# First layer: stored parts of x^T, gains folded into the split of plain weights, and gains of weight sums moved from VectorE to ScalarE

## Chip, cores and metric

The kernel runs on one core of a Trainium2 chip. The metric is the device time of the launch in microseconds (us), the median of several runs. One more run is profiled; its trace gives each instruction's engine, start and length. Short names of the engines: PE is TensorE (PEld its weight loads), DVE is VectorE, ACT is ScalarE, POOL is GpSimd, SP is the queue that issues DMAs.

## What is computed

A trunk of two layers over 2048 frames of width 1024, in float32. Only the first layer is touched:

```
h = rms_norm(x, g)                       # g: a_norm_g, 1024 values
u, v, z = split(h @ w_in, 3)             # w_in: 1024 x 6144
u = gelu(u)
v = layer_norm(gelu(v), ln_g, ln_b)
mixed = einsum('hts,bgshc->bgthc', masked w_s, v in blocks of 128 frames) + b_s
x = x + (u * mixed * silu(z)) @ w_out
```

The second layer (shared K/V, chunked band attention, its output projection) and the final norm follow.

## The kernel before, in words

**Numbers in two parts.** Every float32 operand of a matmul is split into a rounded part `hi` and a remainder `lo`, and a product is three matmuls (`hi*hi`, `hi*lo`, `lo*hi`; lines 114 to 116). A split is an ACT copy that rounds (line 438) and a DVE subtraction (line 441).

**Seven products instead of eight.** `h @ w_in` is cut into column groups `n`: `n = 0, 1` are the halves of `v`, `n = 2` to `5` hold 512 columns of `u` beside 512 of `z`; a last group `"o"` is the projection by `w_out`. In each group the 2 x 2 block product is formed from seven products `ph`, in the order 1, 2, 6, 5, 7, 4, 3, each over eight pairs of row blocks `j`. One (n, ph, j) is a *step*: twelve matmuls of 128 x 512 on PE into one PSUM tile `P`. Groups 0 and 1 share the steps of products 1 and 2 (24 matmuls each). `run_steps` walks through all steps in order; what belongs to other steps (loads, weights, mixing, transposes) is attached to a step number by `at`, `put` and `add_t`.

**Left operands (tiles `S`, six of them).** For group 0 they are made from x^T, scaled by each row's norm (`prep0`), and for products 3 to 7 the split tiles are also stored in DRAM (`hsd`, 512 KB each) by `s_split`. Groups 1 to 5 load products 3 to 7 from `hsd` with `s_load`. For products 1 and 2, groups 2 to 5 load 128 x 512 of plain x^T (tile `xq`, 256 KB, line 676) and split it again (`s_plain`, `s_parts`); the row's norm is then applied at the eviction. `prep` of a step is emitted three steps ahead (`LOOK`).

**Right operands (tiles `T`, eight of them).** `make_t` makes the weights of a product in three functions: `load` (tiles `rw`, tag `raw`, four buffers), `combine` and `finish`. The norm's weight `ga` is multiplied in by `gain`. Products 1, 2 and 3 use one plain block of the weights: two ACT multiplications of 512 columns in place (line 489), then the split: one ACT copy and one DVE subtraction of 1024 columns. Groups 0 and 1 differ: product 1 is `fused` (ACT multiplies straight into `hi`, line 520, and one DVE instruction forms `raw*g - hi`, line 521), and product 2 has its gain on DVE (line 487). Product 6 needs a sum: POOL forms `t1` as a difference of two blocks, `gain` on DVE (line 487) scales it, and POOL subtracts it from a gained third block.

**Who else works on DVE and ACT.** Product 1 is evicted from PSUM by ACT (line 601), the others by DVE (lines 596, 607, 628). For groups 2 to 5 the mixing runs during products 1, 2, 6 and 5: `va` is loaded from DRAM, normalised by four DVE instructions (lines 877 and 878), split (`vh`, `vl`), multiplied on PE (`mx`) and evicted by ACT (line 901). Gated results go through gelu/tanh on ACT, products on DVE or POOL (lines 907, 925, 931, 932), and are transposed on PE (`ty`, line 912).

**What sets the order.** The program is written step by step; a scheduler at compile time then orders each engine's instructions by that priority, by the buffers and by estimated readiness, so a load can be issued well ahead of its step. Each engine and the SP queue then run strictly in their order. `behind`, `in_order` and `paced` add edges that hold one instruction behind another; `last["square"]` is the instruction (the square of a row, line 772) behind which the splits of groups 0 and 1 for products 6, 4, 5 and 7 are held. `row_rep` (line 782) spreads a row's norm for a PE transposition (`rbc`, line 785) that scales x^T in group 0.

Of the kernel before, what the change touches and what calls it, by code (L numbers as in the profile page):

```python
# [33 lines left out]
def trunk_kernel(  # L34
# [20 lines left out]
    nc = tc.nc  # L55
# [331 lines left out]
    with ExitStack() as actx:  # L387
# [3 lines left out]
        NJ = NB // 2  # L391
        hsd = {
            (ph, j): dram.tile([P, 2, 512], F32, name=f"hsd{ph}_{j}")
            for ph in range(3, 8) for j in range(NJ)
        }
        s1d = [dram.tile([P, 512], F32, name=f"s1d{j}") for j in range(NJ)]
        vd = {
# [49 lines left out]
        def comb(o, x_, y_, op=sub):  # L447
            for c in (slice(0, 512), slice(512, 1024)):
                nc.gpsimd.tensor_tensor(o[:, c], x_[:, c], y_[:, c], op=op)
            return o  # L450

        def make_t(n, ph, src, nq, where, chain_of):


            out = [None] * nq
            vs = [None] * nq
            rows = {}
            need = {
                1: [(0, 0)], 2: [(1, 0)], 3: [(1, 1)], 7: [(1, 1), (0, 1)], 4: [(1, 0)],
                6: [(0, 1), (0, 0), (1, 1)], 5: [],  # L460
            }[ph]
            made = n == "o" and ph in (4, 5, 6, 7)
            fused = n in (0, 1) and ph == 1
            if made:
                need = [ph]

            def load(q):
                if made:
                    t = sh.tile([P, 1024], F32, tag="raw", name=f"rw{n}_{ph}_{q}", bufs=4)
                    nc.sync.dma_start(t[:], wod[ph, q][:])  # L470
                    vs[q] = t[:]
                    return
                for r, c in need:
                    t = sh.tile([P, 1024], F32, tag="raw", name=f"rw{n}_{ph}_{r}{c}{q}", bufs=4)
                    nc.sync.dma_start(t[:], src[r, c, q])
                    rows[r, c, q] = t[:]

            def combine(q):
                if made:
                    return  # L480

                def gain(t, r, dve=n in (0, 1) and ph == 2):
                    for i in range(2) if n != "o" and not fused else ():
                        t_ = t[:, i * 512 : i * 512 + 512]
                        k = r * 4 + q * 2 + i
                        if dve:
                            nc.vector.tensor_scalar(t_, t_, ga[:, k : k + 1], None, op0=mul)
                        else:
                            nc.scalar.mul(t_, t_, ga[:, k : k + 1])  # L489
                    return t  # L490

                def raw(r, c):
                    return gain(rows.pop((r, c, q)), r)

                if ph in (1, 2, 3):
                    v = raw(*need[0])
                elif ph == 7:
                    v = raw(1, 1)
                    comb(v, v, raw(0, 1))
                elif ph == 4:  # L500
                    v = chain[n](q)
                    comb(v, raw(1, 0), v)
                elif ph == 5:
                    v = chain[n](2 + q)
                else:
                    if q == 0:
                        chain[n] = chain_of()
                    b22 = raw(1, 1)
                    t1 = comb(chain[n](2 + q), rows.pop((0, 1, q)), rows.pop((0, 0, q)))
                    v = comb(chain[n](q), b22, gain(t1, 0, True))  # L510
                vs[q] = v

            def finish(q):
                out[q] = where(q)
                if fused:
                    for i in range(2):
                        c_ = slice(i * 512, i * 512 + 512)
                        g_ = ga[:, 2 * q + i : 2 * q + i + 1]
                        hi, lo, src = out[q][0][:, c_], out[q][1][:, c_], vs[q][:, c_]
                        nc.scalar.mul(hi, src, g_)  # L520
                        nc.vector.scalar_tensor_tensor(  # L521
                            lo, src, g_, hi.bitcast(F32), op0=mul, op1=sub
                        )
                    return
                ins = split(*out[q], vs[q])
                if n in (0, 1) and ph in (6, 4, 5, 7):
                    behind(ins, last["square"])

            return out, (load, combine, finish)
# [106 lines left out]
        def s_views(t):  # L636
            return [(t[:, 0, k, :], t[:, 1, k, :]) for k in range(4)]
# [8 lines left out]
        def s_parts(n, ph, j, rows):  # L646

            t = s_tile(f"S{n}_{ph}_{j}")
            split(
                t[:, 0].rearrange("p k c -> p (k c)"), t[:, 1].rearrange("p k c -> p (k c)"),  # L650
                rows, "S",
            )
            return t
# [21 lines left out]
                r, c = plain[ph]  # L675
                nc.sync.dma_start(t, xt[2 * j + r, :, c * 512 : c * 512 + 512])

        def s_plain(n, ph, j):
            return s_views(s_parts(n, ph, j, xq.pop((n, ph, j))))


        late = []
        now = [0]
# [95 lines left out]

        def row_rep(blk):  # L780
            d = rep[blk] = acc_tile(f"rp{blk}")[:, 0:P]
            nc.scalar.mul(d, ones[:], rs[:, blk : blk + 1])

        def row_spread(blk):
            tpose(rbc[:, blk, 0], rep.pop(blk), ident[:])
# [177 lines left out]
        for n in range(6):  # L963
            for ph in PH:
                where = in_t(n, ph)
                s = start.get((n, ph), start[0, ph])
                if n == 0 or (n == 1 and ph in (1, 2)):
                    offs = ((-6, 1), (-5, 1), (-4, 1))
                elif n > 2:
                    o = -13 if ph == 6 else -5  # L970
                    offs = ((o, 1), (o, 1), (-5, 1))
                elif ph == 6:
                    offs = ((-13, 3), (-11, 3), (-5, 1))
                elif ph == 4:
                    offs = ((-14, 1), (-12, 1), (-5, 1))
                else:
                    offs = ((-8, 1), (-6, 1), (-5, 1))
                if n == 1 and ph in (1, 2):
                    where = in_big(n, ph, ("hh",) if ph == 1 else ("hl",))
                    offs = ((-5, 1), (-4, 1), (-3, 1))  # L980
                if n == 5 and ph == 3:
                    where = in_big(n, ph, ("hl",))
                add_t(ts, s, n, ph, w_a[n], 2, where, chain_in(n, "hl" if n else "hh"), offs)
# [37 lines left out]
        for n in range(2, 6):  # L1021
# [3 lines left out]
            for r, offs in ((0, (5, 9, 13, 17)), (1, (22, 25, 28, 31))):  # L1025
                for q, o in enumerate(offs):
# [4 lines left out]
                    if r == 0:  # L1031
                        for i in range(2):
                            j = 2 * q + i
                            at(b + 16 + j, lambda n=n, j=j: merge_u(n, j))

        def prep_in(n, ph, j):
            if n == 0:
                return prep0(ph, j)
            if ph in (1, 2):
                return s_plain(n, ph, j)  # L1040
            return s_load(ph, j, n)

        def act_in(s, n, ph, j, views):
# [7 lines left out]
                    evict(m, ph, j, ps, done_uz, uz_c22(m))  # L1051

        for n, ph in start:
            if (n == 0 and ph in (4, 5)) or (n in range(2, 6) and ph < 3):
                for j in range(NJ):
                    at(start[n, ph] + j - LOOK - 2, lambda a=(n, ph, j): xq_load(*a))

# [1011 lines left out]
```

## Time and profile before

| | before |
|---|---|
| median of 3 runs | 2674.11 us (2672.39 to 2676.29) |
| profiled execution, its own time | 2671.83 us |
| its span in the trace | 2670.1 us |
| PE busy | 2595.7 us (97%) |
| DVE busy | 1972.7 us (74%) |
| ACT busy | 1438.0 us (54%) |
| POOL busy | 907.5 us (34%) |
| granted PE clock, mean | 0.994 |
| DMA | 695.14 MB, mean 260 GB/s |

PE is busy nearly all the time, so what there is to be had lies in its idle stretches and in stretches with a lower granted clock. Matmuls overlap, so a row of 0.39 us stands for a matmul that starts about 0.23 us after the one before. All times inside a run are counted from the start of the span. The first layer's column groups 0 to 5 lie between about 8 and 1055 us.

### The profile page before, as it was taken

How to read it: one execution, taken by the hardware profiler on the slowest of the kernel's cores; microseconds unless marked ns; L12 is line 12 of the kernel's file. 1: busy time of each engine (PE TensorE's matmuls, PEld its weight loads, DVE VectorE, ACT ScalarE, POOL GpSimd, SP SyncE). 2: the span in 40 equal slices, each digit the busy share in tenths (PEclk: the TensorE clock that was granted, in tenths of full speed). 3: DMA queues.
4: the chain of work that ended last, by engine and by line, in shares of the span. 5: the costliest groups of instructions: out<-in, count | busy, mean ns of one | idle time of the engine just before them, and what ended most of it. 6: DMA issues, size and time to landing. Idle time of an engine off the chain costs nothing. (4 is left out here: it accounts for less than half of the span.)

```text
span 2670.1 us, 37974 instructions
## 1 busy us (share of the span) xinstructions
PE 2595.7 (97%) x12752; PEld 2161.6 (81%) x12752; DVE 1972.7 (74%) x3060; ACT 1438.0 (54%) x2539; POOL 907.5 (34%) x875
## 2 busy tenths in 40 slices
PE   9899999999999899999999999999999999999997
PEld 7688787878778788888877877888888888888886
DVE  5885795875967968667767766777778777877677
ACT  7453373554734734343356555666666565666564
POOL 3812154242341412302334424334333232232245
PEclk9999999999999999999999999999999999999999
DMA  8799978878778668968867487688788767775667
GB/s 302 282 352 342 362 277 325 305 257 291 259 265 279 230 228 305 331 213 263 297 237 247 163 273 236 220 259 263 247 263 266 232 198 227 254 227 162 200 221 253
DMA packets 273858, 695.14 MB, mean 260 GB/s; under 512 B 28928, under 2 KB 68864, under 8 KB 273664
## 3 DMA queue, kind: packets, MB, share of 16 engines
q1 hardware_dynamic: 273664, 692.72, 76.2%
q8 instruction: 102, 1.67, 0.3%
q14 instruction: 92, 0.75, 0.1%
HBM read 513.82 MB, written 168.30 MB: 255 GB/s over the span
## 5 line engine op out<-in xcount | busy, mean ns | idle before, releaser
L114 PE MATMUL P<-T,S 128*128 128x512 f32 x1248 | 497.0, 398 | 16.7 <-DVE c L607 7.9
L116 PE MATMUL P<-T,S 128*128 128x512 f32 x1248 | 490.1, 393 | 0.4 <-DVE S L441 0.4
L115 PE MATMUL P<-T,S 128*128 128x512 f32 x1248 | 489.1, 392 | 0.3 <-DVE T L521 0.3
L1489 POOL TENSOR_SCALAR pr<-pr,ns 128x640 f32<-128x640 f32 (+4 forms) x256 | 207.7, 812 | 528.5 <-DVE ns L1488 437.5
L114 PE MATMUL pj<-hh_b,wh_b 128*128 128x512 f32 x768 | 319.6, 416 | 0.1
L116 PE MATMUL pj<-hh_b,wl_b 128*128 128x512 f32 x768 | 303.8, 396 | 0.9 <-DVE wl_b L232 0.8
L115 PE MATMUL pj<-hl_b,wh_b 128*128 128x512 f32 x768 | 302.5, 394 | 0.0
L1485 ACT ACTIVATE pr<-pr,ns 128x640 f32<-128x640 f32 (+4 forms) x256 | 195.5, 764 | 188.8 <-DVE ns L1478 187.9
L114 PEld LDWEIGHTS P<-T,S 128*128 128x128 f32 x1248 | 236.3, 189 | 69.2 <-issue 10.2
L116 PEld LDWEIGHTS P<-T,S 128*128 128x128 f32 x1248 | 235.7, 189 | 52.1 <-DVE S L441 1.3
L115 PEld LDWEIGHTS P<-T,S 128*128 128x128 f32 x1248 | 236.4, 189 | 45.4 <-DVE T L521 0.6
L1510 DVE TENSOR_TENSOR pt<-tp,pt 128x640 fp32r<-128x640 f32 (+4 forms) x256 | 188.5, 736 | 44.5 <-ACT pt L1509 41.9
L1478 DVE CUSTOM_DVE_ANT_0 pr<-s,bias 128x640 f32<-128x640 f32 (+4 forms) x256 | 188.1, 735 | 33.8 <-PE s L1470 28.8
L1509 ACT CAST pt<-tp 128x640 fp32r<-128x640 f32 (+4 forms) x256 | 158.7, 620 | 54.8 <-PE tp L1505 50.4
L1505 PE MATMUL tp<-ident,pr 128*128 128x128 f32 x1120 | 166.5, 274 | 9.4 <-DVE pt L1510 7.8
L116 PEld LDWEIGHTS pj<-hh_b,wl_b 128*128 128x128 f32 x768 | 144.5, 188 | 35.4 <-DVE wl_b L232 3.0
L1505 PEld LDWEIGHTS tp<-ident,pr 128*128 128x128 f32 x1120 | 130.6, 141 | 44.3 <-issue 15.8
L1530 PEld LDWEIGHTS pv<-pt,V 128*128 128x128 f32 x896 | 143.0, 188 | 21.0 <-ACT pt L1509 3.6
L114 PEld LDWEIGHTS pj<-hh_b,wh_b 128*128 128x128 f32 x768 | 145.3, 189 | 18.1 <-ACT wh_b L231 1.8
L115 PEld LDWEIGHTS pj<-hl_b,wh_b 128*128 128x128 f32 x768 | 145.4, 189 | 16.1
L1530 PE MATMUL pv<-pt,V 128*128 128x256 f32 (+3 forms) x896 | 153.9, 319 | 2.4 <-ACT pt L1509 1.4
L489 ACT ACTIVATE rw<-rw,ga 128x512 f32<-128x512 f32 x152 | 103.0, 718 | 93.8 <-DMA rw<-in_w_a 88.3
(300 smaller groups left out, 5961.5 us busy)
## 6 DMA issues: line engine op xcount, KB each, us to landing
S<-hsd SPq DMA_DIRECT2D x200, 512.0 KB, 5.4
rw<-in_w_a SPq DMA_DIRECT2D x108, 512.0 KB, 5.9
A<-ytd SPq DMA_DIRECT2D x72, 512.0 KB, 5.8
raw_b<-wk SPq DMA_DIRECT2D x72, 512.0 KB, 4.2
V<-vhd SPq DMA_DIRECT2D x56, 512.0 KB, 5.7
hsd<-S SPq DMA_DIRECT2D x40, 512.0 KB, 6.3
bias<-reld SPq DMA_DIRECT2D x64, 320.0 KB, 4.0
xq<-in_xt SPq DMA_DIRECT2D x72, 256.0 KB, 5.3
```

The lines of the kernel that those rows point to most:

```text
L114: first = mm(ps, lh, rh, start=first, stop=False)
L115: mm(ps, lh, rl, start=False, stop=False)
L116: mm(ps, ll, rh, start=False, stop=last)
L489: nc.scalar.mul(t_, t_, ga[:, k : k + 1])
L1478: nc.vector.tensor_tensor_reduce(out=pr[:, c0:].rearrange("p (a b) -> p a b", a=nseg), in0=ps[:, :nseg, :w], in1=bias[:, c0:].rearrange("p ...
L1485: nc.scalar.activation(pr[:, c0:], pr[:, c0:], AF.Exp, scale=-1.0, bias=nm, accum_out=sl)
L1489: nc.gpsimd.tensor_scalar(pr[:, c0:], pr[:, c0:], sl, 1.0, op0=ALU.mult, op1=ALU.mult)
L1505: ins = tpose(tp[:, b, :], pr[:, b * P : (b + 1) * P], ident[:])
L1509: nc.scalar.copy(oh, tp[:, b0:5, :].rearrange("p a b -> p (a b)"))
L1510: nc.vector.tensor_tensor(pt[:, 2560 + o + b0 * P : 2560 + o + 640], tp[:, b0:5, :].rearrange("p a b -> p (a b)"), oh.bitcast(F32), op=ALU ...
L1530: mm(po[:, q0 * P : q1 * P], vtl[t, p][:, i, hs], rhs, start=(i == blocks[0] and j == 0), stop=(i == 7 and j == 1),)
```

## The change

1. `hsd` also holds products 1 and 2. Group 3 stores its split tiles of product 1 and group 4 those of product 2 (`raw_store`, 16 stores of 512 KB). Group 4 then loads product 1, and group 5 products 1 and 2, from `hsd` (24 loads of 512 KB in place of 24 loads of 256 KB with 24 splits). Both products of group 2, and product 2 of group 3, still load `xq`, split it and store nothing.
2. Plain weights (products 1, 2, 3) of all groups 0 to 5 are `fused`: the gain is multiplied in while splitting.
3. The gain of the sum `t1` in product 6 is on ACT for groups 1 to 5; group 0 keeps it on DVE.
4. `row_rep` becomes the instruction behind which the splits of groups 0 and 1 are held, and the split of product 6 in group 0 is emitted one step later.

```diff
-            for ph in range(3, 8) for j in range(NJ)
+            for ph in range(1, 8) for j in range(NJ)
...
-            fused = n in (0, 1) and ph == 1
+            fused = n != "o" and ph in (1, 2, 3)
...
-                def gain(t, r, dve=n in (0, 1) and ph == 2):
+                def gain(t, r, dve=False):
...
-                    v = comb(chain[n](q), b22, gain(t1, 0, True))
+                    v = comb(chain[n](q), b22, gain(t1, 0, n == 0))
...
-                        g_ = ga[:, 2 * q + i : 2 * q + i + 1]
+                        k = need[0][0] * 4 + 2 * q + i
+                        g_ = ga[:, k : k + 1]
...
-            nc.scalar.mul(d, ones[:], rs[:, blk : blk + 1])
+            ins = nc.scalar.mul(d, ones[:], rs[:, blk : blk + 1])
+            last["square"] = ins.ins.name
...
-                    offs = ((-6, 1), (-5, 1), (-4, 1))
+                    offs = ((-6, 1), (-5, 1), (-3 if (n, ph) == (0, 6) else -4, 1))
...
+        raw_store = ((3, 1), (4, 2))
...
-            if ph in (1, 2):
-                return s_plain(n, ph, j)
+            if (n, ph) in raw_store:
+                return s_split(ph, j, xq.pop((n, ph, j)))
+            if (n, ph) in ((2, 1), (2, 2), (3, 2)):
+                return s_views(s_parts(n, ph, j, xq.pop((n, ph, j))))
             return s_load(ph, j, n)
...
-            if (n == 0 and ph in (4, 5)) or (n in range(2, 6) and ph < 3):
+            if (n, ph) in ((0, 4), (0, 5), (2, 1), (2, 2), (3, 2)) + raw_store:
```

More of the change, by code (lines that the diff above doesn't have):

```diff
@@ L676, in xq_load @@
                 nc.sync.dma_start(t, xt[2 * j + r, :, c * 512 : c * 512 + 512])
-        def s_plain(n, ph, j):
-            return s_views(s_parts(n, ph, j, xq.pop((n, ph, j))))
         late = []
```

## Prediction, made before the changed kernel was run

> **What bounds the kernel now.** I read the page first, then the stretches by time, the waits of PE in them, and last the timeline around the longest of these waits.
>
> ```profile
> span 2670.1 us, 37974 instructions
> PE 2595.7 (97%) x12752; PEld 2161.6 (81%) x12752; DVE 1972.7 (74%) x3060; ACT 1438.0 (54%) x2539; POOL 907.5 (34%) x875
> ```
>
> PE is the bound over the whole; 74.4 us of the span have no matmul. The change touches no matmul, so it can win only part of these, and of what a lower granted clock costs. The products' borders in the trace are the first matmuls of their steps; they give the stretches below: product 1 and 2 of group 3 (511, 536), 1, 2 and 6 of group 4 (693, 723, 750), 1 and 2 of group 5 (875, 903). Two stretches of groups 0 and 1 stand ahead of them for their DMA rates.
>
> ```profile
> core 0: us, PE busy (x) PEld busy (x) DVE busy (x) ACT busy (x) POOL busy (x), PEclk, DMA share, GB/s
> 180.00:240.00 60.00, 60.00 (x266) 49.63 (x266) 41.45 (x62) 21.93 (x34) 5.66 (x4) 1.00 0.94 352
> 300.00:360.00 60.00, 56.89 (x257) 46.55 (x256) 49.38 (x74) 36.56 (x59) 14.58 (x10) 1.00 0.98 372
> 511.00:536.00 25.00, 25.00 (x125) 20.90 (x124) 23.68 (x30) 18.43 (x32) 11.74 (x8) 1.00 0.86 289
> 536.00:570.00 34.00, 28.50 (x123) 22.81 (x122) 29.52 (x28) 20.80 (x37) 20.11 (x14) 0.90 0.81 274
> 693.00:723.00 30.00, 26.97 (x123) 21.82 (x122) 29.96 (x33) 24.78 (x43) 12.95 (x9) 0.94 0.74 246
> 723.00:750.00 27.00, 24.67 (x119) 20.20 (x117) 22.06 (x21) 11.99 (x21) 15.94 (x11) 1.00 0.62 220
> 750.00:777.00 27.00, 26.57 (x121) 22.25 (x122) 19.73 (x24) 11.78 (x21) 6.60 (x5) 0.94 0.64 229
> 875.00:903.00 28.00, 24.66 (x121) 20.13 (x120) 27.96 (x31) 22.32 (x38) 12.85 (x8) 1.00 0.79 263
> 903.00:933.00 30.00, 26.07 (x124) 21.16 (x123) 24.22 (x24) 17.60 (x31) 15.35 (x9) 1.00 0.55 193
> ```
>
> A stretch's loss is its length less PE busy, plus length times the missing clock (after a stop the clock is granted at half for a few us). Group 3: product 2 loses 5.5 + 34 x 0.10 = 8.9 us. Group 4: product 1 3.0 + 30 x 0.06 = 4.8, product 2 2.3, product 6 0.4 + 27 x 0.06 = 2.0. Group 5: 3.3 and 3.9. Together 25.2 us, while DVE is busy 29.96 of 30 in the worst. What PE waited for in the groups 0 to 5 (total, times, longest):
>
> ```profile
> PE P L114 <- DVE c L607: 9.0, 8, 2.4
> PE mx L115 <- DVE vl L441: 5.0, 2, 4.2
> PE ty L912 <- DVE y L932: 4.7, 2, 2.3
> PE P L114 <- DVE x L596: 3.8, 4, 1.8
> PE mx L114 <- ACT m L901: 3.4, 1, 3.4
> PE P L114 <- DMA S<-hsd: 3.1, 2, 2.4
> PE rbc L785 <- ACT rp L782: 2.4, 3, 1.0
> ```
>
> DVE ends most waits; `y` twice for 2.3 us, at the start of group 4 and of group 5. The timeline says what it did instead; first at the start of group 4, then in product 2 of group 5:
>
> ```profile
> 697.35 3.50 POOL L449 TENSOR_TENSOR ch<-rw,rw 128x512 f32<-128x512 f32 x2 [3.95 <-DMA rw<-in_w_a]
> 699.66 1.75 DVE L441 TENSOR_TENSOR S<-xq,S 128x512 fp32r<-128x512 f32 x1
> 701.33 0.68 DVE L932 TENSOR_TENSOR y<-y,c 128x512 f32<-128x512 f32 x1
> 702.15 0.63 PE L912 MATMUL ty<-ident,y 128*128 128x128 f32 x4 [2.34 <-DVE y L932]
> 702.53 1.21 DVE L441 TENSOR_TENSOR T<-rw,T 128x1024 fp32r<-128x1024 f32 x1
> ...
> 926.52 1.84 DVE L877 SCALAR_TENSOR_TENSOR va<-va,lmv,lg 128x512 f32<-128x512 f32 x1 [3.50 <-DMA va<-vd]
> 928.29 0.74 DVE L607 SCALAR_TENSOR_TENSOR c<-P,rs,x 128x512 f32<-128x512 f32 x1
> ```
>
> At 701 the product `y` that PE needs stood behind the subtraction of a split of x^T, stretched to 1.75 us while POOL ran until 700.85. That subtraction goes with the change. At 928 the eviction `c` stood behind an instruction that waited 3.50 us for the load of `va`: this one the change doesn't touch.
>
> **The change part by part.** Durations:
>
> ```profile
> L489 ACT ACTIVATE rw<-rw,ga 128x512 f32<-128x512 f32 x152 | 103.0, 718 | 93.8 <-DMA rw<-in_w_a 88.3 <-issue 4.7 <-ACT th L930 0.7
> L441 DVE TENSOR_TENSOR S<-xq,S 128x512 fp32r<-128x512 f32 x80 | 73.7, 931 | 4.9 <-ACT S L438 4.9
> L441 DVE TENSOR_TENSOR T<-rw,T 128x1024 fp32r<-128x1024 f32 x40 | 55.2, 1395 | 9.9 <-ACT T L438 9.8
> L438 ACT CAST S<-xq 128x512 fp32r<-128x512 f32 x80 | 48.6, 616 | 23.3 <-DMA xq<-s1d 11.0 <-DMA xq<-in_xt 9.7 <-PE P L116 1.2
> L438 ACT CAST T<-rw 128x1024 fp32r<-128x1024 f32 x40 | 41.3, 1048 | 9.5 <-POOL rw L449 4.2 <-PE P L115 3.5 <-DVE rw L487 1.5
> L487 DVE TENSOR_SCALAR ch<-ch,ga 128x512 f32<-128x512 f32 x24 | 17.4, 749 | 7.2 <-POOL ch L449 7.2
> L521 DVE SCALAR_TENSOR_TENSOR T<-rw,ga,T x4: 747/747/752, 8.4 to 10.4; 128x512 fp32r<-128x512 f32 x4
> L607 DVE SCALAR_TENSOR_TENSOR c<-P,rs,x x48: 727/739/752, 63.9 to 940.0; 128x512 f32<-128x512 f32 x48
> ```
>
> *Loads for splits* (product 1 of group 4, both of group 5): per product, eight ACT copies go, 8 x 0.616 = 4.9 us, and eight DVE subtractions, 8 x 0.931 = 7.4 us.
>
> *Fused gains*: per product two ACT copies of 1024 go (2.1 us); the four ACT multiplications stay at about 0.72 us each but write `hi`. On DVE two subtractions (2.8 us) become four instructions of 0.747 (3.0): 0.2 us more. In groups 0 and 1 product 2 also loses its gains on DVE, at a time (31 to 52 us) when PE shows no wait, so I count nothing; if that cover were gone, it is some 3 us of DVE.
>
> *Gain of the sum*: per group DVE loses 4 x 0.749 = 3.0 us and ACT takes 4 x 0.718 = 2.9. It adds a wait to ACT: what stood in DVE for POOL's sum (7.2 us in all) now stands in ACT, with split copies, evictions of product 1 and `m` behind it. Bounds: a gain of 3.0 us per group on one side, a PE wait of up to 7.2 / 5 = 1.4 us per group, were all of it passed on, on the other. I take the gain in DVE time and no wait, as ACT idles 5 us or more in each of these stretches.
>
> So DVE over products 1 and 2 goes from 52.2 of 58 us to 34.7 in group 5 (-14.9 + 0.4 - 3.0), from 52.0 of 57 to 42.0 in group 4, but only from 53.2 of 59 to 50.6 in group 3, which still splits all and in addition stores.
>
> *DMA*. 24 loads grow from 256 to 512 KB and 16 stores of 512 KB come in: 14.7 MB in all. SP gets 16 more issues, and the S loads hold it until a tile of `S` is free:
>
> ```profile
> S<-hsd SPq DMA_DIRECT2D x200, 512.0 KB, 5.4
> hsd<-S SPq DMA_DIRECT2D x40, 512.0 KB, 6.3
> ...
> SPq L641 <- PE P L116: 109.9, 58, 3.2
> SPq L868 <- DVE vl L441: 56.6, 13, 10.1
> ```
>
> The last two rows are SP's own waits from 511 to 945: 109.9 us before 120 S loads, 0.9 us each, up to 3.2. Loads of `va`, weights and the stores of transposes stand behind them. An S tile is free five steps (13.6 us) before its step, a load lands in 5.4, so 8 us are to spare; today's 200 such loads made PE wait 3.1 us in all, both waits where DMA ran at 372 GB/s. At that rate 24 more cost 0.4 us. The eight stores of group 3 lift its product 1 from 289 GB/s by 4.2 MB in 25 us to 457, above the 372. What doesn't fit, (457 - 372) x 25 = 2.1 MB, is 5.7 us late at worst, in front of the `va` loads of product 2. Bounds for group 3: a gain of all 8.9 us, and a loss of 5.7 plus 1.7 for half clock (34 x 0.10 is twice that). With 2.6 us less of 53.2 on DVE little relief gets through, and the late bytes need not be those of `va`. I take 0, where the two small effects meet.
>
> *Order in group 0*: `row_rep` ahead of splits may end part of the 2.4 us of waits for `rp`; between 0 and 2.4 (and 1 us lost, if the later split of product 6 comes late) I take 0.9.
>
> The Trainium skill, page "SBUF — State Buffer", section "SBUF: two separate sides", says that DVE and POOL share one pair of ports as an exclusive lock, and that a DVE instruction with two SBUF inputs is held back by a POOL instruction that reads SBUF. The trace agrees (1.75 us above, and evictions from PSUM never over 0.752). By that rule the fused form is worse: four two-input instructions can each be caught where two were. The 1.395 - 1.21 = 0.18 us by which a subtraction of a weight is longer on average than the free one at 702 would then come twice, some 0.4 us more per product, and the sum would be 1 to 2 us smaller.
>
> **Sum**, from each loss what I expect back:
> - group 4, product 1: 4.0 of 4.8 (the split in front of `y` goes, and with the stop its half clock)
> - group 5, product 1: 2.8 of 3.3 (same pattern)
> - group 5, product 2: 2.3 of 3.9 (what is behind `va` stays)
> - group 4, products 2 and 6: 1.5 of 4.3 (still splits, and stores)
> - group 3: 0 of 8.9; group 0: 0.9
>
> That is 11.5 us. The profiled execution took 2671.83 us (span 2670.1 and 1.7 around it), 2.3 below the median of 2674.11; so 2660.3 for a like execution, and 2662.6 for the median.
>
> **Rivals.** *Full relief*: the weights' earlier readiness clears group 3 too and the evictions in products 2: up to 25.2 + 2.4 = 27.6 us, between 2647 and 2656. For it: DVE ends nearly all waits. Against: two of the long ones hang on `va`.
>
> *Stops move on*: DVE saves time, but waits for the next `va` in its strict order, and PE stops there instead. Left are the two stretched subtractions in front of `y`, 2 x 1.75 = 3.5, less 1 to 2 for S loads behind SP's 10.1 us wait: 2672.
>
> *Slower: DMA crowding.* The stores of group 3 make `va` late by 5.7 us, which stops PE as at 558, with 1.7 of half clock: +7.4. The S loads of groups 4 and 5 come late as where DMA ran at 372 GB/s, 3.1 us per 16 loads: +4.7; and the 3.8 us in products 2 don't come back. -11.5 + 3.8 + 7.4 + 4.7 = +4.4, with S loads late twice as often +9: 2679 to 2683. It decides from a `va` some 5 us late on. Against: at 352 GB/s, from 180 to 240, stores of group 0 run beside a PE without a gap.
>
> **Numbers.** About 0.2% (5 us) is what a measurement here can tell. Likeliest, a part of the relief (2656 to 2668): 0.50. Full relief: 0.20. Stops move on: 0.17. DMA crowding: 0.13, of which a little within 0.2%. Faster 0.70, same 0.18, slower 0.12. The range leaves out about 1 in 20 below and 1 in 8 above: 2647 to 2678; that of the likeliest alone is 2656 to 2668.
>
> **What would show it.** PE idle in 693 to 723 and 875 to 903 under 1 us and full clock there; DVE busy lower by some 10 and 17 us over products 1 and 2 of groups 4 and 5; S loads with PE waits under 2 us; group 3 as before. Wrong, if PE waits for `S<-hsd` in product 1 or 2, if `va` lands later in group 3, or if ACT's wait for POOL's sum shows up as a wait of PE for `S` or `m`.

## The result, and the profile after

| | before | after |
|---|---|---|
| median | 2673.25 us (4 runs beside those of after) | 2643.89 us (2642.95 to 2644.71, 4 runs) |
| ratio, 95% interval | | 0.9891 [0.9874, 0.9909] |
| span of the profiled execution | 2670.1 us | 2641.2 us |

29.4 us faster, where 11.5 were forecast and 2647 was the low end. The page of after:

```profile
span 2641.2 us, 37945 instructions
PE 2583.6 (98%) x12752; PEld 2154.9 (82%) x12752; DVE 1933.1 (73%) x3040; ACT 1411.7 (53%) x2511; POOL 901.8 (34%) x875
```

DVE's busy time fell by 39.6 us over the whole, and PE's idle time went from 74.4 to 57.6 us. PE's busy time fell by 12.1 us with the same 12752 matmuls, because fewer of them ran at a reduced clock (granted 0.994 on average before, 0.998 after). The stretches between first matmuls, product 1 and 2 of group 3, 1, 2 and 6 of group 4, 1 and 2 of group 5 (columns as in the prediction):

```profile
505.00:530.00 25.00, 24.62 (x122) 20.30 (x121) 20.36 (x29) 16.97 (x31) 2.71 (x2) 1.00 0.85 298
530.00:555.00 25.00, 25.00 (x123) 21.11 (x122) 19.23 (x22) 19.56 (x34) 11.34 (x8) 1.00 0.79 300
680.00:705.00 25.00, 25.00 (x125) 20.89 (x124) 13.52 (x19) 15.55 (x28) 4.83 (x5) 1.00 0.86 309
705.00:730.00 25.00, 25.00 (x123) 21.11 (x122) 22.28 (x26) 15.98 (x28) 10.22 (x7) 1.00 0.87 303
730.00:755.00 25.00, 25.00 (x122) 21.03 (x122) 20.32 (x25) 14.70 (x25) 10.67 (x9) 1.00 0.88 334
852.00:877.00 25.00, 25.00 (x124) 20.66 (x123) 12.97 (x18) 14.93 (x27) 6.74 (x5) 1.00 0.90 336
877.00:902.00 25.00, 25.00 (x123) 21.11 (x122) 17.17 (x23) 18.44 (x32) 6.07 (x5) 1.00 0.90 321
```

Six of the seven have no idle PE, and all have full clock. The POOL column is the one the prediction didn't look at: in product 2 of group 3 POOL is busy 11.34 us where it was 20.11, in products 1 and 2 of group 4 15.05 where it was 28.89. POOL's work as a whole is unchanged (901.8 against 907.5 us). It stands elsewhere. PE's waits in the first layer of after, the longest ones (us in total, times, longest):

```profile
PE P L114 <- DVE x L597: 6.7, 6, 2.1
PE ty L911 <- ACT yo L913: 2.3, 1, 2.3
PE P L114 <- DMA S<-hsd: 2.3, 2, 1.4
PE P L114 <- DVE rs L772: 2.1, 1, 2.1
```

Gone are the waits for `c` (9.0 us before), `vl` (5.0), `m` (3.4) and nearly all for `y` (4.7; now 0.4).

To compare many kernels, I use the *loss* of a product: the time from its first matmul to that of the next product, less its number of matmuls times 0.2266 us. Transpositions and mixing matmuls are in it, so 3.0 us stay in products 1, 2 and 6 of groups 3 to 5 (3.0 in product 2 of group 2) in the best case. A loss is that of the one profiled execution, which can be some us off the median (2666.56 against 2663.24 us for "gain later", 2644.86 against 2639.76 for "order and parts 2-4"). Losses in us, with the kernels explained below:

| group, product | before | order 7+4 | order 6+7+4 | part 1 | gain later | parts 2-4 | order and parts 2-4 | after |
|---|---|---|---|---|---|---|---|---|
| 0, 2 | 9.6 | 9.4 | 9.1 | 9.2 | 9.3 | 5.8 | 6.3 | 5.2 |
| 2, 5 | 8.2 | 10.5 | 10.7 | 9.5 | 4.7 | 5.1 | 5.0 | 4.4 |
| 3, 2 | 12.0 | 4.6 | 3.0 | 3.0 | 7.6 | 7.9 | 3.0 | 3.0 |
| 4, 1 | 8.0 | 8.1 | 5.4 | 3.0 | 3.0 | 5.9 | 3.0 | 3.0 |
| 4, 2 | 6.2 | 3.0 | 3.0 | 5.0 | 6.9 | 9.1 | 3.0 | 3.0 |
| 5, 1 | 6.7 | 7.0 | 5.4 | 3.0 | 3.5 | 6.8 | 3.0 | 3.2 |
| 5, 2 | 7.6 | 3.0 | 3.0 | 3.0 | 9.7 | 6.8 | 3.0 | 3.0 |
| sum, first layer with its output projection | 137.8 | 127.8 | 120.2 | 121.9 | 132.5 | 130.1 | 108.9 | 107.4 |
| median of its runs | 2673.25 | 2662.70 | 2654.17 | 2652.97 | 2663.24 | 2668.02 | 2639.76 | 2643.89 |

### The profile page after: what moved, and what is told of

It reads as the page before. It is cut to its first block, busy times and chain, and to the rows that moved or that the text cites. A ratio compares the mean times of both kernels' runs of the same rounds, so it can differ in the third digit from the quotient of the medians.

```text
span 2641.2 us, 37945 instructions
## 1 busy us (share of the span) xinstructions
PE 2583.6 (98%) x12752; PEld 2154.9 (82%) x12752; DVE 1933.1 (73%) x3040; ACT 1411.7 (53%) x2511; POOL 901.8 (34%) x875
## 2 busy tenths in 40 slices
DMA packets 276162, 709.82 MB, mean 269 GB/s; under 512 B 29184, under 2 KB 69120, under 8 KB 275968
## 5 line engine op out<-in xcount | busy, mean ns | idle before, releaser
L114 PE MATMUL P<-T,S 128*128 128x512 f32 x1248 | 494.6, 396 | 14.1 <-DVE x L597 6.7
L1508 PE MATMUL tp<-ident,pr 128*128 128x128 f32 x1120 | 166.6, 275 | 10.7 <-DVE pt L1513 8.2
L232 DVE TENSOR_TENSOR wl_b<-raw_b,wh_b 128x1024 fp32r<-128x1024 f32 x96 | 120.5, 1257 | 28.8 <-ACT wh_b L231 27.9
```

The source lines that it names most:

```text
L114: first = mm(ps, lh, rh, start=first, stop=False)
L232: tv(wl[:], raw[:], wh[:].bitcast(F32), op=sub)
L1508: ins = tpose(tp[:, b, :], pr[:, b * P : (b + 1) * P], ident[:])
```

## Experiments

Each median stands against runs of the kernel before on the same chip; the ratio in brackets is against those, with its 95% interval. Differences in us are to the median of before beside them.

### The four parts, each alone on the kernel before

Part 1 (`raw_store`, loads in `prep_in`, `hsd` for products 1 and 2):

> The kernel before with part 1 alone (16 stores, 24 loads of S in place of splits). Theory A, DVE time: PE's stops in products 1 and 2 of groups 3 to 5 are backlog of DVE, and the late loads of va are part of that backlog, because a va buffer comes free only when DVE has done vl. Then groups 4 and 5, which lose 7.4 and 14.9 us of DVE, lose nearly all of their 16 us of stops, group 3 keeps its 9 us: about 2659 us. Theory B, order: the gain comes from the order that the compile-time scheduler happened to find for the whole change; a part alone gives anything, stops as often gained as lost: within 6 us of before, 2667 to 2679. Theory C, va buffers: stops in products 2 hang on the three va buffers and stay; only product 1 of groups 4 and 5 is cleared, 8 us: 2665.

Measured: 2652.97 us, -19.8 [0.9919, 0.9899 to 0.9940]: faster than all three theories had it.

Part 2 (`fused = n != "o" and ph in (1, 2, 3)`):

> The kernel before with part 2 alone (gain multiplied in while plain weights are split). Theory A, DVE time: DVE time hardly changes in groups 2 to 5 (0.2 us more per product), so 2673 with no more than 2 us either way. Rival A2, the way of the weights: the two ACT copies fewer per product let T and the raw buffers come earlier, and with them the SP queue behind them: 5 to 10 us faster. Theory B, order: within 6 us either way.

Measured: 2663.73 us, -9.0 [0.9972, 0.9958 to 0.9986].

Part 3 (`gain(t1, 0, n == 0)`):

> The kernel before with part 3 alone (gain of the sum t1 on ACT in groups 1 to 5). Theory A, DVE time: 3.0 us of DVE less per group in the stretch with the stops; part of groups 3, 4 and 5 clears, 4 to 9 us faster. Theory B, order: within 6 us either way. Rival: ACT stands still for POOL's sum and PE waits for S or m: 1 to 5 us slower.

Measured: 2676.85 us, +4.1 [1.0011, 1.0002 to 1.0021], as the rival had it. ACT now waits 15.4 us for POOL's sums between 505 and 940 us, and PE waits 10.6 us for `vl` (5.0 in before); that the one causes the other is not shown.

Part 4 (`last["square"]` in `row_rep`, split of product 6 in group 0 one step later):

> The kernel before with part 4 alone (splits of groups 0 and 1 held behind row_rep, split of product 6 of group 0 one step later). All theories: only product 2 of group 0 can change; its loss fell from 9.6 to 5.2 us with the whole change. If this part did it, 3 to 5 us faster and groups 3 to 5 as before; if not, no change.

Measured: 2672.69 us, no change [0.9999, 0.9988 to 1.0011].

What follows: part 1 gives two thirds of the 29.4 us, part 2 another 9.0, against the forecast of nothing for it; alone, the four add up to 24.7. One cell of part 1 can't come from spared splits: it clears product 2 of group 3 (12.0 to 3.0 us), where it removes nothing from DVE and adds stores. What differs there in the trace is POOL: its sums of raw weights for products 7 and 4 of group 3 started 22 to 42 us after product 1's start in the kernel before, inside products 1 and 2 (59 us); with part 1 they start at 37 to 52 us (product 6 starts at 50). The scheduler had put the loads of those raw weights later in SP's order: in group 4 the first of them stood 4 issues ahead of product 2's first x^T load, and in after it stands 9 issues behind. That gives theory D: part 1 works by the order that comes with it. Theory A is that it works by DVE time spared.

### The order alone, DVE time alone, POOL time alone

`b_late`: nothing is removed; the loads of raw weights for products 7 and 4 are held in order behind evictions of product 2 (`ev[n, j]` is that of step (n, 2, j)).

```diff
+        ev = {}
...
-                    nc.sync.dma_start(t[:], src[r, c, q])
+                    ins = nc.sync.dma_start(t[:], src[r, c, q])
+                    if n in (3, 4, 5) and ph in (7, 4):
+                        behind(ins, ev[n, 4 if ph == 7 else 7])
...
+                ev[n, j] = last["evict"]
```

> The kernel before, with nothing removed or added: only the loads of the raw weights for products 7 and 4 of groups 3 to 5 (six per group, and so POOL's eight half-tile sums behind them) are ordered behind evictions of product 2, where before they stand ahead of product 2's first x^T load in SP's queue. Theory D (POOL's sums, early in products 1 and 2, hold DVE's instructions there; the change moved them out): POOL's instructions in that stretch fall from 23, 20, 18 to about 10 to 14 a group, the time by which DVE is held there from about 15 us to 6 to 9 us a group, and the losses of product 1 and 2 of groups 3 to 5 (45 us over bare matmul time, 18 of it kept in every kernel) shrink by 10 to 20 us: 2652 to 2663 us. Theory A (only DVE time taken out by loads and by the fused split counts): no instruction is spared, so 2668 to 2678 us. If the loads come too late, a stop at the first block of product 7 or 4 shows instead.

Measured: 2662.70 us, -10.6 [0.9958, 0.9945 to 0.9971]. The groups of DVE's split subtractions between 505 and 930 us (times, then busy us, mean ns), of before and of this kernel:

```profile
L441 DVE TENSOR_TENSOR S<-xq,S 128x512 fp32r<-128x512 f32 x46 | 48.6, 1065 | 1.0 <-ACT S L438 1.0
```
```profile
L441 DVE TENSOR_TENSOR S<-xq,S 128x512 fp32r<-128x512 f32 x46 | 33.3, 727 | 4.5 <-ACT S L438 4.5
```

The same 46 instructions take 15.3 us less, because POOL no longer runs beside them. The stretching has moved rather than gone: DVE's subtractions `T<-ch` in the same window rise from 1249 to 1591 ns on average, and DVE's busy time over the whole falls by only 9.3 us (1972.7 to 1963.4). In product 2 of group 3 POOL's busy time is now zero:

```profile
538.00:565.00 27.00, 25.82 (x124) 21.41 (x123) 19.91 (x27) 17.44 (x33) 0.00 (x0) 1.00 0.56 208
690.00:720.00 30.00, 26.86 (x122) 21.90 (x121) 26.70 (x34) 20.82 (x35) 7.03 (x5) 0.94 0.56 188
```

The second row is product 1 of group 4, which still loses as before: POOL's four sums for the second half of product 6 (the row at 697.35 in the prediction is two of them) still stand there.

The later loads also leave DMA less busy in product 2 of group 3 (0.56 of its time against 0.81), so a rival says that `va` and x^T simply came earlier. DVE's rows there, of before (536 to 570 us) and of this kernel (538 to 565), speak against it:

```profile
L441 DVE TENSOR_TENSOR S<-xq,S 128x512 fp32r<-128x512 f32 x8 | 9.7, 1218 | 1.0 <-ACT S L438 1.0
L877 DVE SCALAR_TENSOR_TENSOR va<-va,lmv,lg 128x512 f32<-128x512 f32 x4 | 4.0, 1016 | 3.5 <-DMA va<-vd 3.5
```
```profile
L441 DVE TENSOR_TENSOR S<-xq,S 128x512 fp32r<-128x512 f32 x7 | 4.8, 686 | 3.7 <-ACT S L438 3.7
L882 DVE SCALAR_TENSOR_TENSOR va<-va,lmv,lg 128x512 f32<-128x512 f32 x4 | 2.9, 747 | 4.0 <-DMA va<-vd 4.0
```

DVE waits as long for `va` as before (over products 1 and 2 of groups 3 to 5 13.5 us, 14.1 in before), and PE waits for no load between 505 and 930 us in either kernel. What fell is the length of DVE's instructions.

`a_dve`: the kernel after, with the spared DVE time put back.

```diff
+            if ph in (1, 2):
+                d = acc_tile(f"dm{n}_{ph}_{j}")
+                lg, lb = lnw[n]
+                ins = nc.vector.tensor_tensor(d[:], lg[:], lb[:], op=sub)
+                behind(ins, last["evict"])
             return s_load(ph, j, n)
```

> The kernel after, plus one DVE subtraction of 128 x 512 (two constant tiles in, an accumulator tile out that nothing reads) in each step whose split the change had spared: 24 in groups 4 and 5, about 0.75 us each, 18 us of DVE in all. Nothing else is added: no load, no ScalarE copy. Theory A (DVE's time in products 1 and 2 is what the change relieved): the stops of groups 4 and 5 come back in part, +6 to +14 us, 2650 to 2658 us. Theory D (POOL's early sums were the larger half): DVE has slack left, +0 to +4 us, 2643 to 2648 us.

Measured: 2645.63 us (2645.16 to 2646.37) [0.9898, 0.9882 to 0.9914], 1.7 above after, with all of the added DVE time in the trace, in groups 4 and 5:

```profile
L1047 DVE TENSOR_TENSOR dm<-lg,lb 128x512 f32<-128x512 f32 x24 | 18.3, 777 | 0.0
```

`a_pool`: the kernel after, with POOL time added in products 1 and 2.

```diff
+        def dummy(n, ph, j):
+            if n in (3, 4, 5) and ph in (1, 2):
+                d = acc_tile(f"dm{n}_{ph}_{j}")
+                lg, lb = lnw[n]
+                behind(nc.gpsimd.tensor_tensor(d[:], lg[:], lb[:], op=sub), last["evict"])
...
+            dummy(n, ph, j)
```

> The kernel after, plus one POOL subtraction of 128 x 512 (two constant tiles in, an accumulator tile out that nothing reads) per step of products 1 and 2 of groups 3 to 5: 48 in all, 1.0 to 1.8 us each, at most 29 us of POOL a group, roughly what the kernel before had more in that stretch (11, 8 and 7 sums of 1.6 us). Nothing waits for POOL's result. Theory D: DVE is held there as before, some 6 to 12 us a group, and stops of product 1 and 2 return: +6 to +18 us, 2650 to 2662 us. Theory A (POOL off the path costs nothing): 2641 to 2647 us.

Measured: 2675.66 us (2671.01 to 2680.46) [1.0008, 0.9998 to 1.0018]: 31.8 above after, the whole gain gone, with every load and fused split of the change still in place. Theory D had forecast 18 at most. The test puts in more POOL time than before had there: 38.3 and 35.1 us in products 1 and 2 of groups 3 and 4, against 31.9 and 28.9. So it shows that POOL's time in this place is enough to cost the gain, not how much of before's losses it was. The POOL group (46 of the 48 instructions lie between 505 and 930 us), DVE's split subtractions (after: 20 of 799 ns), and products 1 and 2 of group 4:

```profile
L1050 POOL TENSOR_TENSOR dm<-lg,lb 128x512 f32<-128x512 f32 x46 | 78.1, 1724 | 0.0
...
L441 DVE TENSOR_TENSOR S<-xq,S 128x512 fp32r<-128x512 f32 x21 | 23.9, 1146 | 24.4 <-ACT S L438 18.0 <-DMA rw<-in_w_a 6.4
```
```profile
696.00:726.00 30.00, 26.71 (x121) 21.55 (x121) 17.19 (x19) 14.92 (x26) 14.73 (x10) 0.94 0.74 257
726.00:756.00 30.00, 26.02 (x121) 20.32 (x120) 28.89 (x27) 16.79 (x30) 20.39 (x14) 1.00 0.78 269
```

The timeline shows the way at the start of group 4. Five of the added instructions run in a row, and DVE's instructions with two inputs in SBUF take up to 1.78 us beside them; the one that also reads PSUM (`y<-P,y`) takes 0.68. PE then waits for `y`, as it did there in before (2.34 us):

```profile
695.78 8.47 POOL L1050 TENSOR_TENSOR dm<-lg,lb 128x512 f32<-128x512 f32 x5
696.29 1.78 DVE L876 SCALAR_TENSOR_TENSOR va<-va,lmv,lg 128x512 f32<-128x512 f32 x1
698.00 1.75 DVE L930 SCALAR_TENSOR_TENSOR y<-th,y 128x512 f32<-128x512 f32 x1
699.68 0.68 DVE L597 TENSOR_TENSOR y<-P,y 128x512 f32<-128x512 f32 x1
...
701.57 0.63 PE L911 MATMUL ty<-ident,y 128*128 128x128 f32 x4 [3.03 <-DVE y L931]
```

No instruction waits for a result or a buffer of the added ones, and ACT and DVE wait no longer than in after for POOL's own results (22.1 against 31.8 us between 505 and 945 us).

`b_va4`: the kernel before with `bufs=4` for `va`.

> The kernel before with four buffers instead of three for the tiles va of the normalised values. Theory C (va's ring makes product 2 late by itself, so that the prediction's losses behind va are va's own): product 2 of groups 3 to 5 loses 6 to 12 us less, 2661 to 2667 us. Theories A and D (va is late because DVE, which empties the buffers, is behind): within 4 us of before, 2669 to 2677 us.

Measured: 2684.75 us, +11.5 [1.0052, 1.0031 to 1.0073]. Theory C falls: DVE's wait for `va` between 505 and 930 us is shorter (19.1 us against 26.8) and the kernel slower. Why a fourth buffer costs that much is not settled; the losses are in product 5 of group 2 (13.4 us) and product 2 of group 4 (11.8).

### Place against amount

`a_pool57`: the 48 POOL instructions of `a_pool` with `ph in (5, 7)` instead of `(1, 2)`.

> The kernel after, plus the same 48 POOL subtractions as in the run before that put them into products 1 and 2 (+31.8 us), here one per step of products 5 and 7 of groups 3 to 5; nothing reads their results. It tells the place from the amount. Theory D (POOL costs where DVE is the late one, and only by lengthening DVE's instructions there): DVE has slack in products 5 and 7, so +0 to +8 us, 2643 to 2652 us. Rival (48 instructions more in POOL's queue, 80 us, cost by themselves, wherever they stand, because the weights' sums and the merges come late behind them): +15 us or more, above 2659 us.

Measured: 2659.89 us (2650.73 to 2662.70) [0.9937, 0.9915 to 0.9959], 16.0 above after: half the price in this place. The median is at the rival's figure (15 or more), not theory D's, with runs from 2650.73 to 2662.70. The trace shows a cost that neither had named: the added tiles take buffers of the accumulators (`acc_tile`). DVE's evictions wait seven times, 16.9 us in all, for an added instruction to finish, and SP once for 11.7 us, with a store of `ytd` behind it. The copy that needs this store done (`yo`) is late, and PE waits 5.5 us for it in product 3 of group 5, where 7.6 of the 18.5 us of added loss are. In `a_pool` nothing waits for the added instructions. So place and amount aren't cleanly parted here: POOL's time in products 5 and 7 costs 16.0 us with these buffer waits in it, and what it costs without them is not shown.

`a_early`: the kernel after, with the loads and sums of products 7 and 4 asked for early.

```diff
-                    o = -13 if ph == 6 else -5
+                    o = {6: -13, 7: -27, 4: -33}.get(ph, -5)
```

> The kernel after, with nothing added or removed: the loads and the POOL sums of the raw weights for products 7 and 4 of groups 3 to 5 are asked for 22 and 28 steps earlier in the program (during product 1), so that they stand again ahead of most of product 2's x^T loads in SP's queue, as in the kernel before. Theory D: POOL's sums fall into products 1 and 2 again, 18 to 23 POOL instructions there instead of 12, DVE is held 3 to 8 us more a group, and +4 to +15 us, 2648 to 2659 us, in products 1 and 2 of groups 3 to 5. Theory A (only the spared DVE instructions count): 2641 to 2647 us.

In this kernel product 4's sums are written over those of product 6 before product 6 is split, so product 6 of groups 3 to 5 uses other values; the instructions are the same. Measured: 2653.41 us, 9.5 above after [0.9927, 0.9912 to 0.9942]. The time is as theory D expected, but not for its reason: DVE's instructions are hardly lengthened more, and product 2 of group 4 loses 9.0 us with POOL at 20.03:

```profile
707.00:738.00 31.00, 27.99 (x130) 22.64 (x129) 17.31 (x18) 22.65 (x41) 20.03 (x14) 0.97 0.78 278
```

DVE is busy only 17.31 of 31 us. Here it waits for ACT's copies of the splits, which stand in ACT's queue among multiplications of raw weights and copies that wait for POOL's sums. Three rows of its timeline:

```profile
723.94 1.29 DVE L441 TENSOR_TENSOR S<-xq,S 128x512 fp32r<-128x512 f32 x1 [2.15 <-ACT S L438]
...
727.05 3.00 POOL L449 TENSOR_TENSOR ch<-rw,ch 128x512 f32<-128x512 f32 x2 [2.36 <-ACT rw L489]
...
730.08 1.05 ACT L438 CAST T<-ch 128x1024 fp32r<-128x1024 f32 x1 [2.04 <-POOL ch L449]
```

The copy at 730.08 is a split of product 6, and the two sums in front of it are those of product 4, which this kernel has written into the same tile. So ACT's wait comes from the overwriting. In before and after these copies don't wait for product 4's sums (in before the copies start at 722.60 and 726.91, those sums at 727.78). The 9.5 us therefore don't tell theory D from theory A.

`a_late`: the kernel after with `b_late`'s order.

> The kernel after, with the loads of the raw weights for products 7 and 4 of groups 3 to 5 ordered behind evictions of product 2, as in the run that did this to the kernel before (-10.6 us there). After's products 1 and 2 of groups 3 to 5 already lose no more than the 3 us that every kernel has there, so theory D expects little: -2 to +4 us, 2642 to 2648 us (a small gain at product 6 of group 3, 6.3 us, or a small loss at products 7 and 4, whose weights come later). Theory A: the same, no change.

Measured: 2642.82 us [0.9880, 0.9859 to 0.9902]; no difference to after that shows, as both theories expected.

### What is left of part 1, and part 2

`b_late6`: `b_late`, and also the second half of product 6's raw weights later (`ev1[n]` is an eviction of product 1); nothing removed.

```diff
+                    if n in (3, 4, 5) and ph == 6 and q == 1:
+                        behind(ins, ev1[n])
...
+                    ev1[n] = ins.ins.name
```

> The kernel before with nothing removed: beside the loads of products 7 and 4, the three loads of the second half of product 6's raw weights (groups 3 to 5) are ordered behind evictions of product 1, so that POOL's four half-tile sums on them fall 15 us or so later, as they do after the change. Theory D (when POOL's sums fall decides): the stops at the first blocks of product 1 of groups 4 and 5 (8.1 and 7.0 us in the run that ordered products 7 and 4 alone, of which 3 stay in every kernel) shrink, another -4 to -9 us, 2653 to 2659 us. Rival E (those stops belong to the DVE subtractions of the splits that loads replaced): product 1 of groups 4 and 5 stays as it is, 2660 to 2666 us.

Measured: 2654.17 us, -19.5 [0.9933, 0.9917 to 0.9950]: all that part 1 gives alone (2652.97). Products 1 of groups 4 and 5 fall to 5.4 us each, 2.7 and 1.6 less than with `b_late`; part 1 clears them to 3.0. DVE's first instruction on `va` between 505 and 930 us, in before, and here:

```profile
L877 DVE SCALAR_TENSOR_TENSOR va<-va,lmv,lg 128x512 f32<-128x512 f32 x41 | 42.4, 1051 | 26.8 <-DMA va<-vd 26.8
```
```profile
L886 DVE SCALAR_TENSOR_TENSOR va<-va,lmv,lg 128x512 f32<-128x512 f32 x44 | 39.8, 933 | 7.1 <-DMA va<-vd 7.1
```

DVE's wait for the loads of `va` fell from 26.8 to 7.1 us by an order in which nothing of `va` was touched. The gain doesn't need this: in the same window DVE waits 17.9 us for `va` in `b_late`, 16.3 in `a_order` below and 19.6 in after.

`a_order`: parts 2 to 4, and `b_late6`'s order in place of part 1. No x^T part is stored or loaded.

> Parts 2 to 4 of the change without part 1, and in part 1's place the order of the loads of the raw weights for products 6 (second half), 7 and 4 that gave 19.5 us on the kernel before: no x^T part is stored or loaded, every split of products 1 and 2 stays. Parts 2 to 4 alone stand at 2668.0 us. Theory D (part 1 works through that order alone): 2644 to 2651 us, as fast as the change within half a per cent. Rival E (with the rest out of the way, the 24 spared splits count after all): 2652 to 2662 us.

Measured: 2639.76 us (2636.76 to 2644.86) [0.9875, 0.9858 to 0.9893]. It is below theory D's range and as fast as the change (the intervals overlap, so it can't be called faster), with 695.14 MB of DMA instead of 709.82 and all 24 splits in place. Product 1 and 2 of group 4:

```profile
681.00:706.00 25.00, 25.00 (x125) 20.90 (x124) 20.77 (x33) 16.55 (x29) 2.55 (x2) 1.00 0.58 202
706.00:731.00 25.00, 25.00 (x123) 21.11 (x122) 20.30 (x25) 19.19 (x34) 4.30 (x3) 1.00 0.60 213
```

DVE is busy 20.77 us in product 1 where after has 13.52, and PE doesn't stop in either.

`a_nostore`: parts 2 to 4 without part 1 and without that order.

> The kernel after without part 1: products 1 and 2 of groups 3 to 5 are split from plain x^T as in the kernel before, parts 2 to 4 stay. If the parts add up (alone: -20.3 for part 1, -9.5, +3.6, 0), it is 20 us slower than after: 2664 us, within 4. Theory D expects its POOL sums in products 1 and 2 to stand as early as before (18 to 23 a group), rival E that its stops there are those of the kernel before however early they stand.

Measured: 2668.02 us [0.9978, 0.9969 to 0.9988], 24.1 above after. So beside the other parts part 1 is worth 24.1 us, and the order alone 28.3.

`b_gain`: the kernel before; ACT's multiplications of plain weights are held later in ACT's order.

```diff
-                            nc.scalar.mul(t_, t_, ga[:, k : k + 1])
+                            ins = nc.scalar.mul(t_, t_, ga[:, k : k + 1])
+                            if ph in (1, 2, 3):
+                                paced(ins)
```

> The kernel before with nothing removed: only ScalarE's multiplications of the raw weights of products 1, 2 and 3 by norm's weight are ordered behind the evictions issued before them, so that they stand later in ScalarE's queue, not among the evictions of the gating's products. Theory F (part 2 gains because these no longer wait in ScalarE's queue for raw weights, with an eviction behind them that PE waits for): product 5 of group 2 loses 4.4 to 5 us instead of 8.2, ScalarE's idle time on raw weights in group 2 falls from 25 us to under 10, and -3 to -9 us, 2664 to 2670 us. Rival G (part 2 gains by the instructions it saves): 2670 to 2677 us, product 5 of group 2 unchanged. Later multiplications may make a split late, which would show as a stop at the first block of product 2 or 3.

Measured: 2663.24 us, -10.1 [0.9961, 0.9947 to 0.9975]; part 2 alone gave -9.0. The place is in the timeline of the kernel before, two rows of ACT and one of PE in product 5 of group 2:

```profile
432.89 1.33 ACT L489 ACTIVATE rw<-rw,ga 128x512 f32<-128x512 f32 x2 [14.53 <-DMA rw<-in_w_a]
434.13 1.54 ACT L901 ACTIVATE m<-mx,bsh 128x256 f32<-128x256 f32 x4
```
```profile
435.00 0.38 PE L114 MATMUL mx<-vh,ws 128*128 128x256 f32 x1 [3.35 <-ACT m L901]
```

ACT stood 14.53 us before a multiplication whose raw weights hadn't landed; the eviction `m` stood behind it, and PE needed the buffer. ACT's multiplications in group 2 (330 to 505 us) in before, with `b_gain`, and in after:

```profile
L489 ACT ACTIVATE rw<-rw,ga 128x512 f32<-128x512 f32 x30 | 20.3, 717 | 25.7 <-DMA rw<-in_w_a 25.0 <-ACT th L930 0.7
```
```profile
L489 ACT ACTIVATE rw<-rw,ga 128x512 f32<-128x512 f32 x28 | 19.0, 716 | 1.6 <-DMA rw<-in_w_a 1.6
```
```profile
L489 ACT ACTIVATE rw<-rw,ga 128x512 f32<-128x512 f32 x18 | 12.3, 716 | 1.4 <-DMA rw<-in_w_a 1.4
```

28 or 18 of them makes little difference; 25.0 or 1.6 us of waiting in the queue does. That place is 3.5 us of loss. Products 1 and 2 of groups 3 to 5 lose 8.9 us less together, and others 7.1 more. Between 505 and 930 us ACT's wait for raw weights falls too (29.9 to 7.9 us); which of PE's stops there this ended was not followed. The fused form multiplies straight into `T`, whose buffers come free late, and so it is placed late.

`a_nofuse`: the kernel after without part 2.

> The kernel after without part 2: norm's weight is multiplied into the raw weights of products 2 and 3 (and 1 of groups 2 to 5) before the split, as in the kernel before. Forecast on record: part 2 is worth nothing, 2641 to 2647 us. If it is worth beside the others what it gave alone (9.5 us): 2650 to 2656 us, with the loss back mainly in groups 0 to 2 (product 2 and 6 of group 0, product 5 of group 2: 8.2 us against 4.4), where no load was changed.

Measured: 2657.25 us [0.9942, 0.9925 to 0.9959], 13.4 above after; product 5 of group 2 loses 9.4 us.

`a_nosum`: the kernel after without part 3.

> The kernel after without its part 3: the product-6 sum's gain of groups 1 is multiplied by DVE again instead of ScalarE. Alone on the kernel before, part 3 made it 0.11% slower, 3.6 us. If that holds beside the other parts, this kernel is 1 to 4 us faster than after, 2640 to 2643 us; if part 3 pays once the order of the weights' sums is the other one (theory A: DVE work of 3 us a group saved), 1 to 4 us slower, 2645 to 2648 us.

Measured: 2644.86 us [0.9896, 0.9881 to 0.9910]: part 3 is worth nothing that shows.

`a_store2`: `raw_store = ((2, 1), (2, 2))`; groups 3 to 5 load products 1 and 2.

> A version that goes further: products 1 and 2 are stored by group 2, and groups 3, 4 and 5 load all of them (16 splits fewer on ScalarE and DVE in group 3, the same 16 stores, now all in group 2). Group 3's products 1 and 2 lose 3.6 and 3.0 us in the kernel after, of which 3 stay anywhere, so the splits there hide already: -2 to +2 us, 2642 to 2646 us. If the splits are what makes product 6 of group 3 and product 3 of group 2 late (6.3 and 6.4 us): -3 to -6 us. If 16 stores in group 2 crowd its DMA: slower by 2 to 5 us.

Measured: 2650.17 us [0.9913, 0.9899 to 0.9927], 6.3 above after. Products 1 and 2 of group 2 lose 5.8 and 12.6 us (1.5 and 3.0 in after), though the rest improves. The stretch from 300 to 360 us here:

```profile
300.00:360.00 60.00, 55.98 (x254) 45.41 (x252) 39.39 (x68) 28.53 (x50) 9.84 (x8) 1.00 0.99 388
```

DMA is at 0.99 of its time and 388 GB/s, where group 3 of after moves 298 GB/s. That this crowding is what costs is not shown: PE waits for `S<-hsd` are 2.9 us from 285 to 400 us, and product 2, with the larger loss, runs at a DMA share of 0.69 (356 to 391 us). SP waits 28.2 us, ten times, before stores for DVE's splits (325 to 395), and the loads behind them in its order wait too.

## Why the prediction was wrong, point by point

The direction was right, and of the rivals the nearest was full relief (2647 to 2656, chance 0.20). Its reason, weights that are ready earlier, isn't what happened: the raw weights of products 7 and 4 came later. The size of the gain was wrong, by these steps.

**"Group 3: 0 of 8.9".** Measured: 9.0 us less loss in product 2. The step weighed 2.6 us of spared DVE time against late bytes, and took the 29.52 us of DVE in the quoted row as work. In that row POOL is busy 20.11 us, and DVE's split subtractions in it took 1218 ns on average where `b_late`'s take 686. DVE's busy time in products 1 and 2 of group 3 was counted to go from 53.2 to 50.6 us; it went to 39.6, with every split still there. Moving the sums away was enough: `b_late` clears 7.4 us, `b_late6` 9.0, with no instruction less.

**"What is behind `va` stays" (2.3 of 3.9).** Product 2 of group 5 lost 4.6 us less and has no stop. The wait stayed; what it cost went. DVE's wait for `va` in products 1 and 2 of group 5, before and after:

```profile
DVE va L877 <- DMA va<-vd: 5.7, 2, 3.5
```
```profile
DVE va L876 <- DMA va<-vd: 5.3, 2, 3.0
```

So this wait doesn't stop PE by itself. The prediction took the instruction in front of the late eviction for its cause, where DVE was behind already.

**Products 1 of groups 4 and 5 (4.0 and 2.8).** Measured 5.0 and 3.5, so the terms were nearly right, by luck: the reason given ("the split in front of `y` goes") was not needed. `a_order` clears both with the splits in place, and 18.3 us of DVE put back cost 1.7 us. The row at 699.66 doesn't say which of the two was to be taken away, the subtraction or the POOL instruction beside it.

**Fused gains: nothing.** Worth 9.0 us alone, 13.4 beside the other parts. The wait `mx` for `m` (3.4 us) and the 88.3 us that ACT waited for raw weights were both in quoted rows. I counted the instructions' durations and not what stood behind them in ACT's queue. A product's fused subtractions did get dearer for DVE, 4 x 0.796 = 3.2 us in after against 2 x 1.395 = 2.8, but what decided was the queue. The Trainium skill's rule that a POOL instruction reading SBUF holds back a DVE instruction with two SBUF inputs ("SBUF — State Buffer", section "SBUF: two separate sides"), weighed there, would have made the sum smaller by 1 to 2 us. On the lock itself this case's traces agree: 46 subtractions of 1065 ns on average became 727 ns when POOL's work was moved away from them.

**Gain of the sum (3.0 us of DVE per group).** 4.1 us slower alone, nothing beside the others. The wait it adds to ACT was bounded there at 7.2 us over all groups; ACT waits 15.4 us with part 3 alone between 505 and 940 us. DVE's busy time was not the quantity to count.

**Group 0: 0.9.** Product 2 of group 0 lost 4.4 us less in after, 2.2 with part 4 alone, given back elsewhere there.

**DMA and SP.** Right: waits for `S<-hsd` are 2.3 us in total (3.1 before), and group 3's stores did no harm. Group 2's would have (`a_store2`).

Of the chain from part 1's edit to the order I have only the orders themselves: the diff names no load of raw weights, and the scheduler placed them later once the x^T loads and stores were different. `a_pool` shows that stretched DVE instructions alone can cost as much as the whole gain. What share of before's losses in products 1 and 2 runs through them, and what through the multiplications of raw weights that moved later in ACT's queue with the loads, stays open.

## What to carry to other kernels

Where a busy engine is late, first split its time into work and stretch: compare the mean of a group with its shortest instruction, and look at what else ran. A wait in front of a stop isn't yet its cause: see whether the same wait stands elsewhere without a stop. If instructions are stretched or a strictly ordered queue stands before a load, moving the disturbing work by a few steps can be worth as much as removing work. Before crediting an edit with what it removes, make the order that came with it alone: here that gave the whole gain of the stores and loads without one byte more of DMA.

## What was not expected of the hardware

On the same kernel, 24 DVE subtractions in products 1 and 2 of groups 4 and 5 (18.3 us) cost 1.7 us, where 48 POOL subtractions of the same shape in products 1 and 2 of groups 3 to 5 cost 31.8 (POOL's busy time rose by 84.3 us); the same POOL work in two other products cost 16.0, with waits for buffers in it. A POOL subtraction of 128 x 512 took 1.72 us on average where DVE's took 0.78. And a fourth buffer for `va` made the kernel 11.5 us slower.
